# Moving a load-transpose-split step between two stages of a decoder kernel: memory tokens beside the first projections in place of beside the recurrence

## The chip, the cores and the metric

The kernel runs on one core of one Trainium2 chip. The time is the device time in microseconds (us) of one execution of the whole program; a smaller number is better. Five engines of the core matter here: TensorE (PE in the profile, with its weight loads as PEld), VectorE (DVE), ScalarE (ACT), GpSimd (POOL) and SyncE (SP). In this kernel SP computes nothing: it issues nearly all DMA transfers, and it issues them in the order in which they stand in its queue.

## The reference, cut to what matters

The program is one inference step of a two-layer decoder for a prompt of 1024 tokens and 8 sample tokens (one new token each). Layer 0 mixes tokens with a gated linear recurrence (4 heads) and, in parallel, with cross-attention into 256 memory tokens. Layer 1 uses another attention in place of the recurrence. The memory keys and values of both layers are projected once, from the same memory tokens:

```python
mk_p, mv_p = jnp.split(jnp.einsum('bmd,lde->lbme', mem_prompt, w_mem_kv), 2, axis=-1)

def a_mixer(hn, w_in, lb, hg_gain, mem_k, mem_v, w_o, s0):
    q_h, f_h, i_h, g_h, q_m = jnp.split(hn @ w_in, 5, axis=-1)
    q = jax.nn.silu(q_h)...
    logf = jnp.logaddexp(jnp.log(lb), jnp.log1p(-lb) + jax.nn.log_sigmoid(f_h...))
    k = -jnp.expm1(logf)
    v = i_h.reshape(B, L, HG_HEADS, HG_DV)
    o, S = hgrn2_scan(q, k, v, logf, s0)
    o = rmsnorm(o, hg_gain) * jax.nn.silu(g_h)
    om = mem_attend(q_m, mem_k, mem_v)
    out = jnp.concatenate([o, om], axis=-1) @ w_o
```

`mem_prompt` has 256 rows of 1024 numbers; `w_mem_kv` is 1024 by 1024 per layer (512 columns of keys, 512 of values). Everything is float32, and the results are wanted at float32 precision.

## The kernel before, in words

**Tokens and halves.** The 1024 prompt tokens are worked on in two halves of 512; the second half also carries the 8 sample tokens (520 columns). Activations stand transposed: features on the 128 partitions, tokens along the free dimension. In the code the first half is `a0` (layer 0) and `b0` (layer 1), the second `a1` and `b1`.

**Split products.** Every projection is done as three products of rounded numbers: an operand is split into a high part (a cast on ACT) and a low part (a subtraction on DVE), and PE adds high times high, high times low and low times high. `split_w` (L196 to L210) loads a 128x512 block of weights over SP into one of 5 `w` buffers (L201), casts it on ACT (L206) and subtracts on DVE (L207) into one of 5 `ws` buffers. `proj` (L212 to L223) then issues the matmuls (L220) into one of 2 `mm` buffers in PSUM. One head of a projection of the first half takes two such blocks and 24 matmuls.

**Memory tokens.** `mem_load` (L798 to L814) takes the memory tokens in two blocks of 128 rows. Each block comes over SP into a `c` buffer (L803), and is then treated in two groups. A group is four transposes on PE (L807) into the one `ns` bank of PSUM, and then two casts on ACT (L227) and two subtractions on DVE (L228) from that bank into the four `memt` tiles. There is only one `ns` bank, so the transposes of a group can start only when the four splits of the group before them have read it. `mem_keys` (L816) multiplies weight blocks with `memt` (L824, 24 matmuls a head), copies the result out (L829), stores it over SP (L830), transposes it back (L832, L834) and stores that too (L835). `mem_values` (L841) does likewise with L847, L848 and L851. Both need all of `memt` before they are finished, and the values of one layer need it from their first matmul on.

**The recurrence** of the first half is `hgrn_prompt` (L1145). For each of 4 heads it first prepares operands on ACT and DVE (L1158, L1159, L1164), multiplies on PE (L1168) and takes the result out on DVE (L1170, L1171) and decays on DVE (L1150 to L1152). After that come six levels with the matmuls of L1188, and a last part by heads (L1210 to L1237). It is a chain that goes to and fro between PE, DVE and ACT.

**What sets the order.** The program is written as generators, each `yield` being the end of a step. `drain` runs generators to their end, one after the other. `weave((gen, n), (gen, m))` takes steps from its generators in turn, so that each has made the same share of its given count. This order is the priority of the instructions. A planner then lays out one fixed queue for each engine: at each point of its own reckoning it takes the instruction of highest priority that it thinks ready. So an engine's queue can differ from the written order where the planner saw an engine free, but on the chip each engine goes through its queue in order and waits wherever the next instruction is not ready.

Around the change the order is: the value projection of the first half (`a0.v()`, L1042), the gate and query projections (`a0.fq()`: 4 heads of gates with L1073 to L1085 behind each, then 4 heads of queries with L237 to L241 behind each), then the recurrence (`a0.core()`) woven with one chain of memory load, keys, values, keys, values and the first half's memory queries (`a0.qm`).

Of the kernel before, what the change touches and what calls it, by code (L numbers as in the profile page):

```python
# [23 lines left out]
def tile_decoder(  # L24
# [25 lines left out]
    def nm(s):  # L50
        uid[0] += 1
        return f"{s}_{uid[0]}"
# [32 lines left out]
    def T(dt=F32):  # L85
        return tpool.tile([P, WID], dt, tag="t", name=nm("t"))
# [11 lines left out]
    def NS():  # L98
        return nsp.tile([P, 512], F32, tag="ns", name=nm("ns"))
# [18 lines left out]
    def C():  # L118
        return cpool.tile([P, 2, 512], F32, tag="c", name=nm("c"))
# [49 lines left out]
    def drain(*gens):  # L169
        for g_ in gens:  # L170
            for _ in g_:
                pass

    def chain(*gens):
        for g_ in gens:
            yield from g_

    def weave(*streams):

        live = [[0, n, g_] for g_, n in streams]  # L180
        while live:
            cur = min(live, key=lambda e: e[0] / e[1])
            cur[0] += 1
            try:
                next(cur[2])
            except StopIteration:
                live.remove(cur)
# [8 lines left out]
    def split_w(W, k0, nk, m0, alloc=None):  # L196
        out = []
        for a in range(0, nk, 4):
            n = min(4, nk - a)
            raw = wraw.tile([P, 4, P], F32, tag="w", name=nm("w"))  # L200
            nc.sync.dma_start(  # L201
                raw[:, :n, :],
                W[(k0 + a) * P : (k0 + a + n) * P, m0 : m0 + P].rearrange("(k p) m -> p k m", p=P),
            )
            ws = alloc() if alloc else wspl.tile([P, 2, 4, P], F32R, tag="ws", name=nm("ws"))
            nc.scalar.copy(ws[:, 0, :n, :], raw[:, :n, :])  # L206
            nc.vector.tensor_sub(ws[:, 1, :n, :], raw[:, :n, :], ws[:, 0, :n, :].bitcast(F32))  # L207
            for i in range(n):
                out.append((ws[:, 0, i, :], ws[:, 1, i, :]))
        return out  # L210
# [15 lines left out]
    def split_to(dst, src):  # L226
        nc.scalar.copy(dst[0], src)  # L227
        nc.vector.tensor_sub(dst[1], src, dst[0].bitcast(F32))  # L228
# [569 lines left out]
    def mem_load():  # L798
        memt.extend(xpool.tile([P, 2, 2, NM], F32R, tag="x1", name=nm("memt")) for _ in range(ND // 2))
        for tb in range(NM // P):  # L800
            xt = C()
            xf = xt.rearrange("p a n -> p (a n)")
            nc.sync.dma_start(xf, mem_prompt[0, tb * P : (tb + 1) * P, :])  # L803
            for a in range(0, ND, 4):
                ps = NS()
                for k in range(4):
                    nc.tensor.transpose(ps[:, k * P : (k + 1) * P], xf[:, (a + k) * P : (a + k + 1) * P], ident)  # L807
                for b in range(2):
                    d = memt[(a + 2 * b) // 2]
                    split_to(  # L810
                        (d[:, 0, :, tb * P : (tb + 1) * P], d[:, 1, :, tb * P : (tb + 1) * P]),
                        ps[:, 2 * b * P : (2 * b + 2) * P].rearrange("p (k t) -> p k t", k=2),
                    )
            yield  # L814

    def mem_keys(l):  # L816
        for h in range(H):
            w = split_w(w_mem_kv[l], 0, ND, h * P)
            pb = mmp.tile([P, 2, 512], F32, tag="mm", name=nm("mm"))
            ps, pt = pb[:, 0, :], pb[:, 1, :]  # L820
            for k in range(ND):
                wh, wl = w[k]
                for wi, (wt, xi) in enumerate(((wh, 0), (wh, 1), (wl, 0))):
                    nc.tensor.matmul(  # L824
                        ps[:, :NM], wt, memt[k // 2][:, xi, k % 2, :],
                        start=(k == 0 and wi == 0), stop=(k == ND - 1 and wi == 2),
                    )
            src = T()
            nc.scalar.copy(src[:, :NM], ps[:, :NM])  # L829
            nc.sync.dma_start(mks[l][:, h, :], src[:, :NM])  # L830
            for tb in range(2):
                nc.tensor.transpose(pt[:, tb * P : (tb + 1) * P], src[:, tb * P : (tb + 1) * P], ident)  # L832
            tok = T()
            nc.vector.tensor_copy(tok[:, :NM], pt[:, :NM])  # L834
            nc.sync.dma_start(  # L835
                mk_prompt[l, 0, :, h, :].rearrange("(t p) d -> p t d", p=P),
                tok[:, :NM].rearrange("p (t d) -> p t d", t=2),
            )
            yield

    def mem_values(l):  # L841
        pb = mmp.tile([P, 2, 512], F32, tag="mm", name=nm("mm"))
        for k in range(ND):
            raw = wraw.tile([P, 512], F32, tag="w", name=nm("w"))
            nc.sync.dma_start(raw, w_mem_kv[l][k * P : (k + 1) * P, H * P : 2 * H * P])
            ws = wspl.tile([P, 2, 512], F32R, tag="ws", name=nm("ws"))
            nc.scalar.copy(ws[:, 0, :], raw)  # L847
            nc.vector.tensor_sub(ws[:, 1, :], raw, ws[:, 0, :].bitcast(F32))  # L848
            for wi, (xi, i) in enumerate(((0, 0), (1, 0), (0, 1))):
                for tb in range(2):  # L850
                    nc.tensor.matmul(  # L851
                        pb[:, tb, :], memt[k // 2][:, xi, k % 2, tb * P : (tb + 1) * P], ws[:, i, :],
                        start=(k == 0 and wi == 0), stop=(k == ND - 1 and wi == 2),
                    )
            if k % 2 == 1 and k < ND - 1:
                yield
        tok = C()
        nc.scalar.copy(tok, pb)
        nc.sync.dma_start(mv_prompt[l, 0].rearrange("(t p) h d -> p t (h d)", p=P), tok)
        nc.sync.dma_start(mvs[l], tok)  # L860
        yield
# [613 lines left out]
    with tc.issue_after(made[0].ins):  # L1475
# [56 lines left out]
        nc.gpsimd.tensor_tensor(pidx, pidx, iot, op=ALU.add)  # L1532
    drain(head)
    a0 = mixer_a(0, x0)
    drain(a0.v(), a0.fq())
    weave(
        (a0.core(), 22),
        (chain(mem_load(), mem_keys(0), mem_values(0), mem_keys(1), mem_values(1), a0.qm(M)), 22),
    )
    a0.open()  # L1540
    a1 = mixer_a(1, x1)
# [94 lines left out]
```

## Time and profile before

| what | value |
|---|---|
| time, median of 3 runs | 2454.28 us (2452.27 to 2455.25) |
| the profiled execution | 2454.5 us |
| its span, from the first to the last instruction | 2452.8 us |
| PE busy | 2413.3 us (98% of the span) |
| PE weight loads busy | 2161.2 us (88%) |
| DVE busy | 1639.9 us (67%) |
| ACT busy | 1252.4 us (51%) |
| mean granted TensorE clock | 0.998 |
| first half's gate and query matmuls | about 39 to 83 us of the span |
| transposes of the memory tokens | from 84.6 us to 95.5 us |
| recurrence of the first half, PE's part | from 83.3 us to 186 us |

Times inside the span count from its start. PE is shown as busy for nearly all of it, so what can be had is where PE is not busy or where its granted clock is under 1. In the rows of an engine's timeline, the number in brackets at the end is the time the engine stood idle before, and the arrow names what it waited for. In the rows by window, the first number is the length of the window, and then come the busy times of PE, PEld, DVE, ACT and POOL with the number of their instructions, the granted clock, the busy share of the DMA engines and their GB/s.

### The profile page before, as it was taken

To read this page: it belongs to the slowest core of one execution; us is meant where nothing else is said; L and a number is where in the kernel's file an instruction comes from. 1 tells how busy PE (TensorE), PEld (TensorE's weight loads), DVE (VectorE), ACT (ScalarE), POOL (GpSimd) and SP (SyncE) were. 2 spreads that over 40 slices of the span, in tenths; PEclk is the share of its full clock that TensorE was granted. 3 is DMA by queue.
4 is the path that set the end of the run, shared out by engine and by line. 5 is a ranking of instruction groups with operands and counts; after the bars stand their busy time and mean duration, and the time that the engine had idled before them with its cause. 6 is when DMAs were issued, how large, how long until landed. Compare 5 with 4: busy or idle time off the path is not lost.

```text
span 2452.8 us, 42098 instructions
## 1 busy us (share of the span) xinstructions
PE 2413.3 (98%) x15839; PEld 2161.2 (88%) x15839; DVE 1639.9 (67%) x2987; ACT 1252.4 (51%) x2441; POOL 187.0 (8%) x315
## 2 busy tenths in 40 slices
PE   8999999999999999999999999999999999999998
PEld 6888889888879988999999989877777888999998
DVE  5766557665797686664756685788688467755565
ACT  5547644354445554555434554555554445654445
POOL 1000101111000000111200102121000100000000
PEclk9999999999999999999999999999999999999999
DMA  6354676567645447676766649745354563464542
GB/s 190 100 174 110 157 197 161 135 171 204 204 137 166 132 147 235 176 188 161 190 172 168 199 132 291 206 146 154 95 164 120 145 191 116 144 194 141 151 143 74
DMA packets 534733, 397.40 MB, mean 162 GB/s; under 512 B 21325, under 2 KB 473018, under 8 KB 534530
## 3 DMA queue, kind: packets, MB, share of 16 engines
q1 hardware_dynamic: 505346, 315.02, 43.2%
q0 software_dynamic: 29184, 79.70, 14.2%
q8 instruction: 124, 2.03, 0.3%
q14 instruction: 79, 0.65, 0.1%
HBM read 364.81 MB, written 101.14 MB: 190 GB/s over the span
## 4 chain that ended last, share of the span: by engine, by line
PE 84%; DVE 6%; DMA 5%; issue 2%; ACT 2%; POOL 0%; SPq 0%; DVEq 0%; ACTq 0%; POOLq 0%
PE mm L220 44%; PE q L511 13%; PE q L648 9%; PE q L464 3%; PE mm L1042 2%; PE s L1188 1%; DMA c<-in_cache_mem_v 1%; PE s L1385 1%; PE s L906 1%; PE mm L824 1%; PE mm L851 1%; PE q L680 1%; PE s L1351 1%; PE s L875 1%; DVE ws L207 1%
## 5 line engine op out<-in xcount | busy, mean ns | idle before, releaser
L220 PE MATMUL mm<-x,ws 128*128 128x260 f32 (+1 forms) x6240 | 1113.6, 335 | 4.9 <-DVE t L237 1.7
L220 PEld LDWEIGHTS mm<-x,ws 128*128 128x128 f32 x6240 | 941.8, 188 | 125.8 <-issue 2.4
L206 ACT CAST ws<-w 128x512 fp32r<-128x512 f32 (+1 forms) x652 | 382.3, 588 | 489.5 <-PE mm L220 337.0
L207 DVE TENSOR_TENSOR ws<-w,ws 128x512 fp32r<-128x512 f32 (+1 forms) x652 | 418.9, 648 | 246.8 <-ACT ws L206 241.7
L220 PE MATMUL mm<-m,ws 128*128 128x512 f32 (+1 forms) x1344 | 281.8, 361 | 0.1
L220 PEld LDWEIGHTS mm<-m,ws 128*128 128x128 f32 x1344 | 217.9, 189 | 36.8 <-issue 1.0
L648 PE MATMUL q<-m,ws 128*128 128x260 f32 (+1 forms) x1824 | 221.8, 283 | 0.0
L648 PEld LDWEIGHTS q<-m,ws 128*128 128x128 f32 x1824 | 218.9, 188 | 1.2 <-DVE t L534 0.4
L502 DVE TENSOR_TENSOR ws<-w,ws 128x512 fp32r<-128x512 f32 x181 | 124.0, 690 | 86.6 <-ACT ws L501 83.6
L501 ACT CAST ws<-w 128x512 fp32r<-128x512 f32 x181 | 111.8, 621 | 110.2 <-PE q L648 35.6
L511 PE MATMUL q<-x,ws 128*128 128x260 f32 (+1 forms) x1188 | 158.1, 282 | 0.0
L511 PEld LDWEIGHTS q<-x,ws 128*128 128x128 f32 x1188 | 148.7, 188 | 0.0
L511 PE MATMUL q<-y,ws 128*128 128x260 f32 x912 | 119.7, 284 | 0.4 <-ACT q L521 0.3
L511 PEld LDWEIGHTS q<-y,ws 128*128 128x128 f32 x912 | 113.7, 189 | 0.8 <-ACT q L521 0.5
L464 PE MATMUL q<-x,ws 128*128 128x260 f32 (+1 forms) x720 | 91.3, 284 | 0.2 <-DVE r L400 0.2
L464 PEld LDWEIGHTS q<-x,ws 128*128 128x128 f32 x720 | 88.4, 189 | 1.8 <-DVE r L400 0.5
L511 PE MATMUL q<-a,ws 128*128 128x260 f32 (+1 forms) x672 | 87.0, 282 | 0.0
L511 PEld LDWEIGHTS q<-a,ws 128*128 128x128 f32 x672 | 83.2, 188 | 0.0
L657 DVE TENSOR_TENSOR r<-r,q 128x260 f32<-128x260 f32 (+1 forms) x128 | 48.5, 420 | 50.5 <-PE q L648 50.5
L237 DVE TENSOR_SCALAR t<-mm 128x512 f32<-128x512 f32 (+1 forms) x58 | 40.1, 691 | 48.0 <-PE mm L220 47.8
L563 POOL COPY mk<-a 128x1 f32<-128x1 f32 x36 | 21.3, 592 | 645.5 <-ACT a L1241 392.9
L228 DVE TENSOR_TENSOR m<-t,m 128x512 fp32r<-128x512 f32 (+1 forms) x88 | 60.8, 691 | 9.4 <-ACT m L227 8.7
(355 smaller groups left out, 3029.5 us busy)
## 6 DMA issues: line engine op xcount, KB each, us to landing
w<-in_w_gu SPq DMA_DIRECT2D x297, 256.0 KB
w<-in_w_down SPq DMA_DIRECT2D x160, 256.0 KB
wsum<-in_w_gu POOLq DMA_DIRECT2D x72, 512.0 KB, 6.6
w<-wsum SPq DMA_DIRECT2D x104, 256.0 KB
w<-in_w_in_a SPq DMA_DIRECT2D x80, 256.0 KB
w<-in_w_o SPq DMA_DIRECT2D x64, 256.0 KB
wsum<-in_w_gu POOLq DMA_DIRECT2D x24, 640.0 KB, 7.3
wsum<-wsum POOLq DMA_DIRECT2D x24, 512.0 KB, 5.7
```

The costliest lines, as they stand in the source:

```text
L206: nc.scalar.copy(ws[:, 0, :n, :], raw[:, :n, :])
L207: nc.vector.tensor_sub(ws[:, 1, :n, :], raw[:, :n, :], ws[:, 0, :n, :].bitcast(F32))
L220: nc.tensor.matmul(ps[:, a, : PW[g]], wt, xt[k][:, xi, o : o + PW[g]], start=(k == 0 and wi == 0), stop=(k == nk - 1 and wi == 2),)
L228: nc.vector.tensor_sub(dst[1], src, dst[0].bitcast(F32))
L237: nc.vector.tensor_scalar(sv(x, g), pv(ps, g), -44.0, None, op0=ALU.max)
L464: ins = nc.tensor.matmul(pp[a][:, :h], wt, xt[k][:, xi, a * h : (a + 1) * h], start=(k == 0 and wi == 0), stop=(k == ND - 1 and wi == 2),)
L501: nc.scalar.copy(w[:, 0, :], src)
L502: nc.vector.tensor_sub(w[:, 1, :], src, w[:, 0, :].bitcast(F32))
L511: nc.tensor.matmul(ps[:, :h], w[:, wj, k * P : (k + 1) * P], x[:, xi, :], start=(first and k == 0 and wi == 0), stop=(k == 3 and wi == 2), ...
L648: nc.tensor.matmul(pp[a][:, :h], wt, mids[k][:, xi, a * h : (a + 1) * h], start=(k == 0 and wi == 0), stop=(k == nf - 1 and wi == 2),)
L657: nc.vector.tensor_add(d, d, pp[a][:, :h])
L1042: nc.tensor.matmul(pb[i][:, a, :], xt[k][:, xi, c * P : (c + 1) * P], ws[:, s, :], start=(k == 0 and wi == 0), stop=(k == ND - 1 and wi == 2),
```

## The change

`mem_load()` is taken out of the chain that is woven with the recurrence. It is woven with the gate and query projections instead, one of its two blocks for every four of their eight steps. With the counts given, the first block stands after the first gate head and the second after the fifth step (the first query head). The other weave keeps its remaining 20 steps, and its count goes from 22 to 20. No instruction is added or removed.

```diff
-    drain(a0.v(), a0.fq())
+    drain(a0.v())
+    weave((a0.fq(), 8), (mem_load(), 2))
     weave(
         (a0.core(), 22),
-        (chain(mem_load(), mem_keys(0), mem_values(0), mem_keys(1), mem_values(1), a0.qm(M)), 22),
+        (chain(mem_keys(0), mem_values(0), mem_keys(1), mem_values(1), a0.qm(M)), 20),
     )
```

## The prediction

> **What bounds the kernel now.** I read the page first, then the busy time by windows, then PE's own timeline where a window showed PE short.
>
> ```profile
> span 2452.8 us, 42098 instructions
> ...
> PE 2413.3 (98%) x15839; PEld 2161.2 (88%) x15839; DVE 1639.9 (67%) x2987; ACT 1252.4 (51%) x2441; POOL 187.0 (8%) x315
> ```
>
> PE is busy for all but 2452.8 - 2413.3 = 39.5 us of the span. An edit that leaves PE's work as it is can win only from those 39.5 us, and from stretches at a lower clock. The windows around the change:
>
> ```profile
> core 0: us, PE busy (x) PEld busy (x) DVE busy (x) ACT busy (x) POOL busy (x), PEclk, DMA share, GB/s
> 39.00:83.00 44.00, 44.00 (x192) 35.79 (x191) 28.45 (x46) 28.82 (x49) 0.00 (x0) 1.00 0.32 96
> 84.00:88.00 4.00, 1.40 (x11) 1.17 (x10) 4.00 (x11) 2.99 (x8) 0.00 (x0) 1.00 0.23 69
> 88.00:92.00 4.00, 3.34 (x14) 3.01 (x13) 2.24 (x6) 1.76 (x6) 0.00 (x0) 0.59 0.02 4
> 92.00:96.00 4.00, 3.35 (x23) 2.89 (x23) 3.42 (x9) 1.53 (x5) 0.00 (x0) 0.98 0.00 0
> 96.00:100.00 4.00, 4.00 (x33) 3.79 (x32) 3.82 (x10) 2.99 (x9) 0.00 (x0) 1.00 0.01 3
> ...
> 84.00:100.00 16.00, 12.09 (x75) 10.86 (x74) 13.48 (x35) 9.27 (x27) 0.00 (x0) 0.89 0.06 19
> 100.00:116.00 16.00, 16.00 (x132) 15.70 (x132) 15.44 (x40) 4.70 (x11) 0.00 (x0) 1.00 0.59 161
> ```
>
> The first row is the stage that the step moves to: PE never stops, DVE and ACT are idle for a third of it. Then the projections end, and from 84 to 100 us PE is short by 16.00 - 12.09 = 3.91 us, with the granted clock down to 0.59 in one of those four windows. PE's timeline names the waits (the last bracket is the idle time before the row and what ended it):
>
> ```profile
> 83.27 1.47 PE L1168 MATMUL s<-b,a 128*128 128x192 f32 x8
> 84.57 0.60 PE L807 MATMUL ns<-ident,c 128*128 128x128 f32 x4
> 87.77 0.63 PE L807 MATMUL ns<-ident,c 128*128 128x128 f32 x4 [2.60 <-DVE memt L228]
> 89.06 2.93 PE L1168 MATMUL s<-b,a 128*128 128x192 f32 x8 [0.66 <-ACT b L1164]
> 91.78 0.78 PE L807 MATMUL ns<-ident,c 128*128 128x128 f32 x4
> 93.02 0.51 PE L824 MATMUL mm<-memt,ws 128*128 128x256 f32 x2 [0.46 <-ACT memt L227]
> 93.72 1.22 PE L824 MATMUL mm<-memt,ws 128*128 128x256 f32 x8 [0.19 <-DVE memt L228]
> ```
>
> 2.60 + 0.66 + 0.46 + 0.19 = 3.91, so these four waits are the whole gap. Three of them are for the memory tokens: the second group of transposes waits until the splits of the first have left the one `ns` bank, and the key matmuls wait for `memt`. Meanwhile the key weights stand ready, and nothing else on PE is.
>
> **The price of the low clock.** The chain of waits gives the same eight matmuls of L1168 at both clocks, and two paces that I need below:
>
> ```profile
> 89.06 2.94 PE s L1168 x8
> ...
> 95.26 0.44 PE ns L807 x4
> ...
> 100.06 1.37 PE s L1168 x8
> ...
> 104.85 2.90 PE mm L824 x24
> ```
>
> 2.94 - 1.37 = 1.57 us. From the windows it is 3.34 x 0.41 + 3.35 x 0.02 = 1.44. I take 1.5. That the hole of 2.60 us is its cause is read from the order of the rows: the clock was 1.00 through the hole and low right after it. A smaller hole elsewhere did not do it:
>
> ```profile
> 540.00:560.00 20.00, 18.27 (x89) 14.60 (x89) 15.96 (x21) 8.36 (x15) 2.67 (x2) 1.00 0.85 243
> ```
>
> ```profile
> 557.43 4.79 PE L220 MATMUL mm<-x,ws 128*128 128x260 f32 x38 [1.73 <-DVE t L237]
> ```
>
> So after the change, holes of up to 1.73 us should leave the clock alone. [...]
>
> **The change, part by part.** *Removed from 84 to 97 us.* Sixteen transposes (L807, four groups at 0.44, 1.8 us of PE), eight casts and eight subtractions:
>
> ```profile
> L228 DVE TENSOR_TENSOR memt<-ns,memt 128x256 fp32r<-128x256 f32 x8 | 3.3, 414 | 0.6 <-ACT memt L227 0.6
> L227 ACT CAST memt<-ns 128x256 fp32r<-128x256 f32 x8 | 3.0, 369 | 5.5 <-PE ns L807 4.6 <-DVE memt L228 0.7
> ```
>
> *Added from 44 to about 72 us.* The same. On PE the 1.8 us are a wash: PE is full there, so what leaves one place is paid in the other. On DVE and ACT 3.3 and 3.0 us go into idle time of 44.00 - 28.45 = 15.55 and 44.00 - 28.82 = 15.18 us, so they cost nothing if the weight splits keep their lead. Without that cover they would cost 3.3 us at most.
>
> *Is there cover for PE at 83 us?* The splits made by then:
>
> ```profile
> L207 DVE TENSOR_TENSOR ws<-w,ws 128x512 fp32r<-128x512 f32 x20 | 13.8, 688 | 9.3 <-ACT ws L206 9.3
> L206 ACT CAST ws<-w 128x512 fp32r<-128x512 f32 x20 | 12.4, 621 | 14.0 <-PE mm L1042 6.7 <-PE mm L220 5.0 <-DMA w<-in_w_in_a 1.6
> ```
>
> These are the groups up to 83.4 us. The gate and query heads need 8 x 2 = 16 of the 20, so 4 blocks of key weights stand split, each good for 12 matmuls: 4 x 12 x 2.90 / 24 = 5.8 us of work that waits for `memt` alone. With `memt` there early, PE has more ready work than the 3.91 us that it idled, and each block it uses sets a `ws` buffer free some 10 us sooner than now. DVE then makes the next block in 0.69 us (13.8 / 20) against 1.45 us that PE needs for one.
>
> *The queues.* The loads of the memory tokens are moved in the order too, and so stand ahead of the weight loads of the gates. SP's queue and its waits:
>
> ```profile
> 10.39 0.91 SPq L803 DMA_DIRECT2D c<-in_mem_prompt  x2
> ...
> 60.46 19.20 SPq L201 DMA_DIRECT2D w<-in_w_mem_kv  x8
> 82.06 3.12 SPq L845 DMA_DIRECT2D w<-in_w_mem_kv  x2
> 99.12 0.33 SPq L830 DMA_DIRECT2D mks<-t  x1
> 99.60 0.33 SPq L845 DMA_DIRECT2D w<-in_w_mem_kv  x1
> ```
>
> ```profile
> SPq L830 <- ACT t L829: 19.3, 4, 13.9
> ```
>
> SP issued the two token loads at 10.39 us already, 34 us before the transposes could now want them, so I cost the loads at nothing; the `c` buffers they hold are freed sooner, not later. After 85.2 us SP stood for 13.9 us behind the store of the first key head (L830), with all weight loads behind it. That store comes sooner when the first key head does, so this wait shortens. POOL's queue is not touched: it has no instruction from 39 to 100 us.
>
> *New waits.* Two kinds that the trace does not price. First, the bank wait of the second group of each token block now stands in the projections' queue, where a stopped PE costs in full. Lower end: 0 each, as the planner may put projection matmuls between. Upper end: 2.60 each, the row above. Second, PE must take the key matmuls and the recurrence's first part by turns, and can stand before a head of L1168 that is not ready: from 0 (no wait from 96 to 100 us, where both alternate) to 0.66 for each of three heads. The nearest row for queues that were interleaved and miss by a little is the memory attention's:
>
> ```profile
> PE s L899 <- DVE b L892: 2.1, 7, 0.6
> ```
>
> 0.3 us a wait. I take 2 x 0.3 = 0.6 and 3 x 0.3 = 0.9, together 1.5, with 0 and 2 x 2.60 + 3 x 0.66 = 7.2 as ends.
>
> **The sum.** The profiled execution took 2454.5 us, 1.7 more than its span, and 0.2 more than the median of 2454.28. From 2454.3: minus 3.91 for the idle time, minus 1.5 for the clock, plus 1.5 for new waits gives 2450.4 us, 0.16% less. From no change a measurement of this kernel can tell about 0.2%, 4.9 us: under 2449.4 is faster, over 2459.2 slower. With the new waits at 0 the time is 2448.9. Holes in the rest of the program, 39.5 - 3.9 less 10.3 in the first 20 us (PE is busy for 9.71 us there), come to 25.3 us and may shift by 2 us or so when the planner's queues shift; that is a guess of size, not a row.
>
> ```profile
> 0.00:20.00 20.00, 9.71 (x48) 7.52 (x49) 12.92 (x36) 12.54 (x27) 6.74 (x27) 1.00 0.72 237
> ```
>
> **Rivals.**
> *All of it is won.* No new wait, and the later holes don't grow: 2448.9 us. For it: 5.8 us of split key weights against a gap of 3.91. Against: every change between engines in the rows above left some wait.
> *DVE sets the pace.* From 84 to 100 us DVE is busy 13.48 of 16, and from 100 to 116 us 15.44 of 16. If the recurrence and the key splits are held up by DVE, PE's hole closes early and opens again later, and only DVE's relief of 3.3 us is won: 2451.0 us. Against: PE is at 16.00 of 16.00 next to that full DVE.
> *The low clock stays.* The rows show it after the hole, not because of it. If it is not the hole's doing, only 3.91 - 1.5 is won: 2451.9 us. Against: the other windows above without such a hole have 1.00. [...]
> *The projections stall (slower).* The planner puts the second group of transposes close behind the first, and on the chip the four splits stand behind the gates' own chain on ACT and DVE. Then both waits are 2.60 us, each with its low clock of 1.5: 2454.3 - 5.4 + 0.9 + 8.2 = 2458.0 us. It decides from 5.4 - 0.9 = 4.5 us of such stalls on. For it: one `ns` bank, and 2.60 us once already. Against: here PE has 24 matmuls a head to put between, and at 89 us it did so with L1168. Anything worse than this, two longer stalls, passes 2459.2.
> *It does nothing.* The planner takes instructions when it thinks an engine free, and could leave the transposes about where they were: 2454.3 us. Against: they now rank ahead of seven projection heads, and their data is there.
>
> **Chances.** 2450.4 (0.44: 0.12 below 2449.4, 0.32 within 0.2%; its own range 2448.9 to 2452.5), all won 0.23 (faster), DVE's pace 0.10, the low clock stays 0.05, nothing 0.06 (all three within), stalls 0.12 (0.09 slower, 0.03 within). Faster 0.35, within 0.2% 0.56, slower 0.09. The range goes from 2447.0, all won and 2 us of later holes, to 2455.5, past the cases without stalls; I leave out most of the stalls and the luckiest shifts, under 2 in 10.
>
> **What would show it.** L807 between 44 and 72 us in groups of four among the rows of L220, with idle time before the second and fourth group of 0 to 0.6 us. From 39 to about 85 us PE without other holes, the end of the projections some 1.8 us later. Behind them L824 at once beside L1168, PE over 15 of 16 us busy in the next 16, and clock 1.00. SP's wait at L830 well under 13.9 us. The forecast is wrong if PE waits for L228 inside the projections by more than 1 us, if the low clock remains, or if a new hole stands between 100 and 220 us. From 100 to 330 us PE now waits for this alone, in the memory attention behind 230 us:
>
> ```profile
> PE s L899 <- DVE b L892: 0.6, 3, 0.2
> ```

## The result, and the profile after

The changed kernel takes 2446.55 us (median of 7 runs, 2445.13 to 2449.87); the kernel before, run beside it, 2455.08 us. The ratio is 0.9968, with a 95% interval of 0.9956 to 0.9979: faster by 0.32%, or 8 us, with 5 to 11 us as the bounds. The forecast was 2450.4 us, 0.16%, and gave "within 0.2%" the largest chance. The direction was right, the size was half of what was measured, and the median lies just under the range's low end of 2447.0.

The busy time by windows of the changed kernel, with the columns as before:

```profile
39.00:83.00 44.00, 43.99 (x199) 35.35 (x198) 30.15 (x52) 29.71 (x56) 0.00 (x0) 1.00 0.31 90
...
84.00:100.00 16.00, 16.00 (x116) 15.27 (x115) 14.55 (x35) 10.11 (x26) 0.00 (x0) 1.00 0.42 126
100.00:116.00 16.00, 16.00 (x111) 14.75 (x111) 14.95 (x39) 4.39 (x8) 0.00 (x0) 1.00 0.54 162
```

PE has no hole from 84 to 100 us any more (16.00 against 12.09 us busy), and its clock is 1.00. The projections stay full too. PE's timeline shows why:

```profile
45.36 0.60 PE L807 MATMUL ns<-ident,c 128*128 128x128 f32 x4
45.72 2.79 PE L220 MATMUL mm<-x,ws 128*128 128x512 f32 x11
48.51 0.63 PE L807 MATMUL ns<-ident,c 128*128 128x128 f32 x4
48.90 19.90 PE L220 MATMUL mm<-x,ws 128*128 128x512 f32 x85
68.63 0.60 PE L807 MATMUL ns<-ident,c 128*128 128x128 f32 x4
68.98 2.79 PE L220 MATMUL mm<-x,ws 128*128 128x512 f32 x11
71.78 0.63 PE L807 MATMUL ns<-ident,c 128*128 128x128 f32 x4
72.17 14.35 PE L220 MATMUL mm<-x,ws 128*128 128x512 f32 x61
86.35 1.47 PE L1168 MATMUL s<-b,a 128*128 128x192 f32 x8
87.52 3.13 PE L824 MATMUL mm<-memt,ws 128*128 128x256 f32 x24
```

Eleven projection matmuls (2.79 us) stand between the two groups of each token block, about as long as the second group waited for the `ns` bank before (2.60 us). No row has an idle time in brackets. At 87.52 us a whole key head runs at once. SP's wait behind the first key head's store fell from 13.9 us to 4.6 at most:

```profile
SPq L830 <- ACT t L829: 11.2, 5, 4.6
```

**Where the 8 us are.** Two marks of PE stand in both kernels: the first projection matmul (L220) and the transposes of the sample tokens (L339), behind the recurrence. In the kernel before, and then in the changed one:

```profile
38.91 2.47 PE L220 MATMUL mm<-x,ws 128*128 128x512 f32 x10
```

```profile
216.06 0.66 PE L339 MATMUL s<-ident,c 8*128 8x8 f32 x8
```

```profile
39.83 5.70 PE L220 MATMUL mm<-x,ws 128*128 128x512 f32 x24
```

```profile
210.64 0.66 PE L339 MATMUL s<-ident,c 8*128 8x8 f32 x8
```

From mark to mark it is 177.15 us before and 170.81 after: 6.3 us of the 8.2 by which the two spans differ. The first mark came 0.9 us later, and the rest of the program is 2.8 us shorter. The queues of all engines behind L339 hold the same instructions in the same order in both kernels, so those 2.8 us need another reason; the runs below look for it. Within the stretch, the time from each PE matmul's start to the next one's, summed by line (worked out from the trace's rows), moves like this:

| line | before | after | difference |
|---|---|---|---|
| L807, transposes of the memory tokens | 6.16 | 1.48 | -4.68 |
| L1168, recurrence's first part | 6.43 | 4.74 | -1.69 |
| L824, keys | 24.37 | 23.53 | -0.84 |
| L220, projections | 84.02 | 85.01 | +0.99 |
| all other lines | 56.18 | 56.05 | -0.13 |

By place: from the first L220 row to the first row of L1168 (83.27 us before, 86.35 after) the changed kernel takes 2.2 us more, and from there to L339 it takes 8.5 us less. Of the 0.99 on L220, 0.69 lies among the gate and query matmuls; the other 0.3 lies later, where no transpose of the memory tokens stands in either kernel.

### The profile page after: what moved, and what is told of

Its sections match the earlier page's. It is cut to its first block, busy times and chain, and to the rows that moved or that the text cites. A ratio compares the mean times of both kernels' runs of the same rounds, so it can differ in the third digit from the quotient of the medians.

```text
span 2444.6 us, 42106 instructions
## 1 busy us (share of the span) xinstructions
PE 2412.0 (99%) x15839; PEld 2159.3 (88%) x15839; DVE 1639.0 (67%) x2987; ACT 1251.2 (51%) x2441; POOL 186.1 (8%) x315
## 4 chain that ended last, share of the span: by engine, by line
PE 87%; DVE 6%; DMA 3%; issue 2%; ACT 2%; POOL 0%; SPq 0%; DVEq 0%; ACTq 0%; POOLq 0%
PE mm L220 46%; PE q L511 13%; PE q L648 9%; PE q L464 3%; PE mm L1042 2%; PE s L1188 1%; PE s L906 1%; PE s L1385 1%; PE mm L851 1%; PE mm L824 1%; PE s L875 1%; PE q L680 1%; PE s L1351 1%; DVE ws L207 1%; DMA b<-qd 1%
## 5 line engine op out<-in xcount | busy, mean ns | idle before, releaser
L220 PE MATMUL mm<-x,ws 128*128 128x260 f32 (+1 forms) x6240 | 1115.6, 335 | 3.5 <-DVE r L657 1.7
L220 PEld LDWEIGHTS mm<-x,ws 128*128 128x128 f32 x6240 | 941.0, 188 | 123.9 <-DVE x L228 2.1
L220 PE MATMUL mm<-m,ws 128*128 128x512 f32 (+1 forms) x1344 | 281.8, 361 | 0.5 <-DVE r L400 0.4
L220 PEld LDWEIGHTS mm<-m,ws 128*128 128x128 f32 x1344 | 217.8, 188 | 37.2 <-issue 1.0
L566 POOL DMA_DIRECT2D wsum<-in_w_gu x64 | 58.5, 935 | 114.1 <-DMA wsum<-wsum 89.5
```

The source lines that it names most:

```text
L220: nc.tensor.matmul(ps[:, a, : PW[g]], wt, xt[k][:, xi, o : o + PW[g]], start=(k == 0 and wi == 0), stop=(k == nk - 1 and wi == 2),)
L566: nc.gpsimd.dma_start(d, a, accum_op=ALU.add)
```

## The experiments

Each kernel was compared with the kernel before on its own chip. As single executions scatter by several us, I read the stretch from L220 to L339 in the profile as well, in which two profiles of the same kernel agree within 0.5 us: 177.2 and 177.7 for the kernel before, 170.8 and 170.9 for the changed one. The stretches below are taken from the starts of those two rows.

| kernel | ratio to before, 95% interval | L220 to L339, us |
|---|---|---|
| the change | 0.9968 (0.9956 to 0.9979) | 170.8 |
| filled hole | 0.9994 (0.9983 to 1.0004) | 175.7 |
| three banks | 1.0002 (0.9990 to 1.0014) | 176.4 |
| half moved | 0.9976 (0.9967 to 0.9986) | 172.6 |
| more transposes | 1.0022 (1.0012 to 1.0032) | 178.3 |
| load put back | 0.9984 (0.9974 to 0.9993) | 171.9 |
| one stage earlier | 0.9977 (0.9965 to 0.9988) | 168.7 (transposes ahead of it) |
| forced stall | 1.0001 (0.9991 to 1.0010) | 176.4 |
| no weave | 0.9980 (0.9971 to 0.9990) | 170.4 |

**Both kernels again.** No edit.

> The kernel before once more, to see what repeats. If the hole behind the projections belongs to the queues, PE is again short by 3.9 us (3.7 to 4.1) from 84 to 100 us, and the low clock stands there again if the hole causes it. The later differences between the two first profiles (1.5 us near 557 us, 0.7 us near 1480 us, 0.8 us near 1850 us, 3.0 us together) stand behind instructions whose order is the same in both kernels. Theory: they are chance of transfers, so this second profile of the same kernel differs from the first by 0.5 to 3 us in those places. Rival: they come from the change in some way that the order does not show, and then the same kernel repeats them within 0.3 us each.

> The changed kernel once more. Theory: PE has no hole from 84 to 100 us and its clock is 1.00 there; between the start of the projections' matmuls (L220) and the transposes of the sample tokens (L339) it takes 6.3 us less than the kernel before (6.0 to 6.6). The start of L220 may lie up to 1 us off the first profile in either direction, if that difference of 0.9 us is chance. Rival for the later places: the hole near 550 us is again 0.3 us and not above 1 us, if the change closed it.

The hole came back with three of its four waits (2.60, 0.67 and 0.46 us; the one of 0.19 did not), and so did its absence. The second pair differs by 6.8 us in the stretch, a little more than the 6.0 to 6.6 expected. In the later places the same kernel did not repeat itself. The hole of 1.73 us at 557 us was 0.66 in this profile of the kernel before:

```profile
558.03 5.98 PE L220 MATMUL mm<-x,ws 128*128 128x260 f32 x48 [0.66 <-DVE t L237]
```

In the changed kernel it was 0.28 and then 0.36, as the rival asked. But the kernels below, in which PE has the same order there, show anything from 0.58 to 3.52, so the change did not close it. From L339 to PE's last matmul it took 2229.6 and 2230.8 us before, 2226.9 and 2229.2 after, and the eight kernels below lie between 2227.7 and 2234.4. So the 2.8 us between the first two profiles are within what this part varies by itself; that the change adds something there isn't shown. The waits at 557 us go back to transfers: in the chain of waits of the first profile stand 7.85 us for a store of the sample states and 4.12 us for a load. The start of L220 was 40.1 us in this profile of before and 39.4 in that of after, the other way round than in the first pair, so that 0.9 us was chance too. One thing differed in the stretch: the low clock held for two windows where it had held for one.

```profile
88.00:92.00 4.00, 2.38 (x8) 2.01 (x9) 2.89 (x7) 2.05 (x7) 0.00 (x0) 0.56 0.02 7
92.00:96.00 4.00, 3.54 (x17) 3.02 (x16) 2.86 (x9) 0.76 (x3) 0.00 (x0) 0.59 0.01 4
```

**The hole filled, for the clock.**

```diff
+                if tb == 0 and a == 0:
+                    pj = S()
+                    for j in range(12):
+                        nc.tensor.matmul(pj, onesr, x0[j % ND][:, 0, :G], start=True, stop=True)
                 for b in range(2):
```

> The kernel before, with 12 matmuls of 512 columns that nobody reads behind the first group of the memory tokens' transposes, where PE stood for 2.60 us. They take 12 x 0.233 = 2.8 us. Theory that the hole causes the low clock: the clock stays 1.00 from 88 to 92 us, the next eight matmuls of L1168 take 1.4 us and not 2.9, and from 83 to 100 us the kernel is some 1.3 us quicker (1.5 for the clock less the 0.2 by which the filling is longer than the hole). Rival that the low clock is not the hole's: it remains 0.5 to 0.6 there, L1168 takes 2.9 us, and the kernel is 0.2 us slower. In the whole time neither can be told from 0 (0.1%).

```profile
85.64 3.03 PE L811 MATMUL s<-x,onesr 128*128 128x512 f32 x12
88.50 0.62 PE L807 MATMUL ns<-ident,c 128*128 128x128 f32 x4
89.33 1.57 PE L1172 MATMUL s<-b,a 128*128 128x192 f32 x8 [0.22 <-ACT b L1168]
```

```profile
88.00:92.00 4.00, 3.31 (x19) 2.29 (x17) 3.36 (x11) 1.95 (x7) 0.00 (x0) 1.00 0.01 4
```

With useless work in the hole the clock stays 1.00, the eight matmuls (here L1172) take 1.57 us in place of 2.93, and the stretch is 1.4 us shorter although PE does more. So the hole causes the low clock, at the price that was forecast.

**Three banks in place of one.**

```diff
-                ps = NS()
+                ps = S()
```

> The kernel before, with the memory tokens' transposes written into the three banks that the recurrence also uses, and not into the one ns bank. Theory that the one bank makes the hole: the second group follows the first at once, the wait of 2.60 us before it is gone, and with it the low clock: 3 to 4 us less. Rival that the chain behind it makes the hole (transposes, then eight casts and subtractions one behind the other, and only then key matmuls): the hole moves behind the second group, PE is short by 3 us or more from 84 to 100 us as before, and the gain is under 1 us.

```profile
85.89 0.63 PE L807 MATMUL s<-ident,c 128*128 128x128 f32 x4 [0.80 <-DVE b L1171]
88.87 2.22 PE L1168 MATMUL s<-b,a 128*128 128x192 f32 x8 [2.35 <-ACT b L1164]
```

The rival holds. The wait of 2.60 us is gone from the second group, and one of 2.35 us stands behind it, with the low clock (0.70 from 88 to 92 us). The stretch is 0.8 us shorter. So the bank named the wait, but it wasn't the reason: what came next on PE had to wait until ACT and DVE had gone through their queues. The test isn't a clean one, as the recurrence uses the three banks too (the wait of 0.80 us) and the third and fourth group stand behind L1168 in PE's queue.

**Half of it moved.**

```diff
-    drain(a0.v(), a0.fq())
+    drain(a0.v())
+    ml = mem_load()
+    weave((a0.fq(), 8), (islice(ml, 1), 2))
...
-        (chain(mem_load(), mem_keys(0), ..., a0.qm(M)), 22),
+        (chain(ml, mem_keys(0), ..., a0.qm(M)), 21),
```

> Only the first block of memory tokens is moved beside the projections; the second stays beside the recurrence. Theory that PE stood for want of ready work: key matmuls need both blocks, so PE still has none at 83 us and has to wait for the splits of the second block. With half the transposes and splits left, the hole is about half: 1.5 to 2.5 us idle from 84 to 100 us, and the gain is 2 to 3.5 us. Rival that the single bank alone counts: the wait between the first two groups is moved away and one between the last two is left, 2.4 us with other work beside it, so nearly all of the 6.3 us is won.

```profile
87.66 0.50 PE L824 MATMUL mm<-memt,ws 128*128 128x256 f32 x2 [0.79 <-ACT memt L227]
88.44 1.33 PE L824 MATMUL mm<-memt,ws 128*128 128x256 f32 x9 [0.28 <-DVE memt L228]
89.61 0.60 PE L807 MATMUL ns<-ident,c 128*128 128x128 f32 x4
```

The stretch is 4.6 us shorter, above the 2 to 3.5 expected, and 1.07 us of idle time is left. A key matmul takes one of the eight feature blocks of `memt`, and the planner ran those that were ready between the two last groups. With holes of 0.8 us the clock stays 1.00. The theory missed that the second block alone does not empty PE; the rival, which had nearly all of the 6.3 us won, missed the 1.07 us.

**More transposes, for their price.**

```diff
+                for _ in range(4):
+                    pj = S()
+                    for k in range(4):
+                        nc.tensor.transpose(pj[:, k * P : (k + 1) * P], xf[:, (a + k) * P : (a + k + 1) * P], ident)
```

> The changed kernel with each group of transposes followed by four more of the same that nobody reads, 16 groups (64 transposes) added beside the projections. It prices what a group costs on a full PE. By the pace inside a group (0.44 us) they add 16 x 0.44 = 7.0 us to the changed kernel. By what the first profile of the changed kernel shows, where each group takes 0.37 us and the projections lost another 0.25 us at each change between transposes and matmuls, they add 6 to 7 us if the groups stand together and 10 us if they stand apart. If the projections had idle time on PE, they would add clearly less than 6 us.

The 16 groups cost 178.3 - 170.9 = 7.4 us in the stretch, 0.46 each; they stood nearly together, and 0.45 us of the 7.4 are two waits for the `ns` bank. In the changed kernel the four groups stand apart and cost 1.48 on L807 and 0.69 on the projections around them, which is 0.54 each. So what moved is not free in its new place, and is no wash with 1.8 us either: it costs 2.2. In the whole time this kernel is 10 to 13 us above the changed one and those close to it (1.0022 against 0.9968 to 0.9980). What goes beyond the 7.4 us lies outside the stretch; a longer hole at 557 us, shown in the last section, is one part of it, and the rest is open.

**DVE's and ACT's load put back** into the changed kernel, for the rival that DVE sets the pace:

```diff
             nc.sync.dma_start(mks[l][:, h, :], src[:, :NM])
+            if l == 0:
+                for j in range(2):
+                    mj = M(F32R)
+                    split_to((mj[:, 0, :NM], mj[:, 1, :NM]), src[:, :NM])
```

> The changed kernel with eight casts and eight subtractions of 128x256 put back on ACT and DVE beside the recurrence, two of each behind every key head of layer 0, into tiles that nobody reads. So DVE and ACT have about the load back that the change took from them (3.3 and 3.0 us), and PE has nothing back. Theory that PE sets the pace there and DVE's relief is worth nothing: the time is that of the changed kernel, within 1 us from L1168 to L339. Rival that DVE sets the pace: up to 3.3 us slower than the changed kernel.

The stretch is 1.0 us longer than that of the changed kernel. The increase lies on L824 (24.79 against 23.53 by the sums of starts), and PE has no idle time between L1168 and L339 in either kernel. But PE's queue is not the same any more: with the added instructions the planner cut the key heads into pieces, where the changed kernel runs each as 24 matmuls at once.

```profile
91.23 3.62 PE L824 MATMUL mm<-memt,ws 128*128 128x256 f32 x28
95.65 0.42 PE L824 MATMUL mm<-memt,ws 128*128 128x256 f32 x1
96.47 3.02 PE L824 MATMUL mm<-memt,ws 128*128 128x256 f32 x23
```

By the whole time its interval overlaps that of the changed kernel. So DVE does not set the pace: with its load back, PE waits for nothing. Whether the 1.0 us comes from that load or from the other order of PE's queue is not shown.

**One stage earlier.**

```diff
-    drain(a0.v())
-    weave((a0.fq(), 8), (mem_load(), 2))
+    weave((a0.v(), 4), (mem_load(), 2))
+    drain(a0.fq())
```

> The memory tokens one stage earlier still: woven with the value projection. The transposes then stand between 20 and 37 us. Theory: PE is full there too, so the time is that of the changed kernel within 1 us, 6 us less than before; the hole at 84 us is closed in the same way. Rival: the splits meet the weight splits of the value projection, which have little lead there (each weight block is cast when its transfer lands), and PE waits for them: 1 to 3 us slower than the changed kernel.

From the first value matmul (L1042) to L339 it takes 195.5 us, against 195.9 and 195.6 in the two profiles of the changed kernel and 201.9 before. So between the two stages ahead that were tried the place does not matter. The earlier one brings no more either: PE is busy for 23.4 of the 24 us from 16 to 40 us in this kernel as in the kernel before.

**Stalls forced into the projections**, the slower rival of the prediction as a kernel:

```diff
-    weave((a0.fq(), 8), (mem_load(), 2))
+    fq, ml = a0.fq(), mem_load()
+    for n in (1, 4):
+        for _ in range(n):
+            next(fq)
+        next(ml)
+        with tc.issue_after(moved[0].ins):
+            next(fq)
+    drain(fq, ml)
```

Here `moved[0]` is the last transpose that `mem_load` issued.

> The changed kernel, with the next head's matmuls put behind the second group of each token block on PE's queue. So PE has nothing to put between the two groups and must stand until the four splits of the first have left the ns bank, twice, in the projections. This is the slower rival of the prediction, made on purpose. Each hole should be 2.3 to 2.7 us by the profile and cost 0.2 us more than that, as the end of the last matmul before it is shown inside its busy time. Theory that any such hole brings the low clock: 2 x (2.7 + 1.5) = 8.4 us more than the changed kernel from L220 to L339. Rival, that one hole of this length alone does not bring it (before, the hole stood in 4 us in which PE was busy for only 1.40 us): 5.4 us more, the clock stays 1.00.

```profile
44.56 0.60 PE L807 MATMUL ns<-ident,c 128*128 128x128 f32 x4
47.71 0.63 PE L807 MATMUL ns<-ident,c 128*128 128x128 f32 x4 [2.55 <-DVE memt L228]
...
80.80 0.63 PE L807 MATMUL ns<-ident,c 128*128 128x128 f32 x4 [1.43 <-DVE memt L228]
```

```profile
48.00:52.00 4.00, 4.00 (x15) 3.15 (x13) 2.61 (x6) 1.68 (x4) 0.00 (x0) 0.59 0.23 66
52.00:56.00 4.00, 4.00 (x19) 3.26 (x18) 0.69 (x1) 1.09 (x2) 0.00 (x0) 0.98 0.13 35
```

The first hole is as forecast and brings the low clock. Into the second the planner drew eight matmuls of the recurrence (L1168), which left 1.43 us of it, and the clock stayed. The stretch is 5.6 us longer than in the changed kernel: 2.55 + 1.43 idle and about 1.5 of clock. Nearly the whole gain is given back, at a ratio of 1.0001. So the rival's mechanism is real, and one full stall costs about what it said (2.55 and 1.5 us); the order on PE's queue decides whether it comes.

**Without the weave.**

```diff
-    drain(a0.v())
-    weave((a0.fq(), 8), (mem_load(), 2))
+    drain(a0.v(), mem_load(), a0.fq())
```

> The changed kernel, but with the memory step written as a whole between the value projection and the gate projections and not woven with them. Theory: the planner spreads the groups by itself, as the matmuls of the first gate head are ready while the bank is not, so the time is that of the changed kernel within 1 us (170.9 us from L220 to L339, less up to 0.5 us for a group that falls before L220). Rival that the weave keeps the groups apart: holes of up to 2.6 us between the groups, 2 to 5 us slower than the changed kernel.

```profile
39.96 0.60 PE L807 MATMUL ns<-ident,c 128*128 128x128 f32 x4
40.31 2.79 PE L220 MATMUL mm<-x,ws 128*128 128x512 f32 x11
42.94 0.60 PE L807 MATMUL ns<-ident,c 128*128 128x128 f32 x4
```

The planner spreads the groups by itself, with eleven matmuls between, and the stretch is 170.4 us. The weave is not what kept PE full; the ready matmuls were.

## Why the prediction was right and wrong

*The hole, right in place and cause.* PE's 3.91 us of idle time from 84 to 100 us were for work that the memory tokens hold back, and all of it went. Three banks did not help, half the move won 4.6 us, and every version with the tokens ahead of 83 us and no forced stall won 6 to 7: the reason is that PE had nothing else ready. I named the bank in the same breath as the reason; that part fell.

*The clock, right.* 1.5 us forecast, 1.4 measured by filling the hole. The rival "the low clock stays" is out. In the windows of the first profile of before, 0.41 x 4 + 0.02 x 4 = 1.7 us of clock are lost. In its trace that is one stretch of 3.41 us at 0.50, from 88.72 to 92.13 us; the second profile lost twice that, 0.44 x 4 + 0.41 x 4 = 3.4 us. Idle time of 2.55 us brought the low clock in the forced stall too.

*New waits, the step that failed first.* I took 1.5 us for two bank waits and three waits of the recurrence, by the row of the memory attention. They are 0: eleven matmuls fitted into each bank wait, and L1168 and L824 alternate from 86 to 104 us without one. In another order of the same queue such waits do come: the forced stall has 2.55 and 1.43 us of them, against the upper end of 2.60 each.

*The sum's idle term, mis-sized.* Behind the projections the sum took away 3.91 us of idle time, 1.5 for the clock and 1.8 for the transposes: 7.2 us. From the first row of L1168 to L339 it was 8.5. About 0.7 of the 1.3 us that are missing lies on the transposes: their 6.16 us less 3.72 of idle time and 4 x 0.44 of pace. The idle time of a row begins at the end of the last matmul, and a group of transposes fills 0.60 us in the timeline and 0.44 in the chain, so a wait costs some 0.2 us more than it shows. Most of the rest lies on the key matmuls (0.84 less 0.19 of idle time), which stood in small pieces before; no run takes that apart. *The wash, wrong:* 1.8 us forecast for the transposes in the projections, 2.2 measured. Together 8.5 - 2.2 = 6.3 us, where the sum without new waits has 3.91 + 1.5 = 5.4.

*Cover and queues, right.* The split weights were there, SP's longest wait at L830 fell from 13.9 to 4.6 us, and ACT and DVE took the splits without a wait on PE.

*DVE's pace*, 0.10 of the chance, is not borne out: with the load back the stretch grew by 1.0 us of the 3.3, and PE had no wait there.

*The range.* From 2454.3 us the stretch alone gives 2448.0, or 0.26%. That is already beyond 0.2%; with waits of 0 my own sum gave 2448.9, and that case should have had the larger chance. What lies between 6.3 us and the measured 8 is not settled: the interval of 5 to 11 us holds both, and the rest of the program varies by more. The two kernels with the same gain in the stretch, one stage earlier and no weave, came out only 5 to 6 us below the kernel before, so part of the 8 may be chance.

## What to carry to other kernels

Where one engine is full everywhere but in one hole, look for what that hole's work waits for, and move its small preparations into the stage ahead, where other engines have idle time; both stages ahead that were tried had it (DVE was busy for 28.45 of 44 us in the one and for 12.76 of 24 us in the other) and won 6 to 7 us. A bank or semaphore named at the hole need not be its reason: ask what else the engine had ready. Price a hole by the starts of the instructions on both sides, and add the clock where PE does little around it: here 1.7 us, behind a step of 3.41 us in which PE was busy for 0.63 us.

## What the hardware showed that was not expected

The length of a hole alone does not decide whether the low clock follows. One and the same wait stands near 1694 us in the kernel before and near 1687 us in the changed one. The rows are from the second profile of the kernel before, from its first, and from the second of the changed kernel:

```profile
1694.96 1.16 PE L1385 MATMUL s<-b,a 128*128 128x128 f32 x8 [1.79 <-ACT b L1382]
```

```profile
1693.48 1.16 PE L1385 MATMUL s<-b,a 128*128 128x128 f32 x8 [1.55 <-ACT b L1382]
```

```profile
1687.18 1.16 PE L1385 MATMUL s<-b,a 128*128 128x128 f32 x8 [1.95 <-ACT b L1382]
```

After 1.79 us the clock was 0.57 in the next window; after 1.55 it was 1.00, as after 1.73 at 557 us, and it was 1.00 after 1.95 too, the longest of these. What the traces show in its place is a fixed step of time. From the first record of the clock on, it changes only at whole steps of 3.41 us in all twelve traces, and it stays low for one step or two. In the first profile of the kernel before the record begins at 13.63 us; the clock falls at 88.72, 22 steps on, is 0.50 for one step, and then 1.00 for 690 steps, until it falls at the end. In that of the changed kernel it is 1.00 for 710 steps, from 16.57 to 2440.03 us. Two such steps each, from the second profile of the kernel before and from the second of the changed kernel:

```profile
1692.71:1696.12 3.41, 1.62 (x11) 1.15 (x11) 2.91 (x5) 2.59 (x5) 0.00 (x0) 1.00 0.82 276
1696.12:1699.53 3.41, 3.41 (x10) 2.41 (x8) 2.52 (x4) 1.15 (x2) 1.61 (x2) 0.50 0.23 85
```

```profile
1683.51:1686.93 3.42, 1.72 (x8) 1.07 (x6) 3.42 (x6) 1.52 (x3) 0.00 (x0) 1.00 0.62 173
1686.93:1690.34 3.41, 3.05 (x17) 2.27 (x18) 2.91 (x5) 2.00 (x5) 0.51 (x1) 1.00 0.64 215
```

The hole of 1.95 us lay across two steps. Up to the last 15 us of the program, the clock fell after each of the seven steps at full clock in which PE was busy for less than 1.5 us (0.63 us from 85.31 us on, in the first profile of the kernel before), after one of the five with 1.5 to 1.9, and after none with more. (At the program's very end it fell after more: after 2.03 us in the first profile of the kernel before, where PE had only the transposes of L753 and the matmuls of one column of L768.) So in these traces the share of a step that PE is busy goes with the fall, and a hole of some 2 us cost its length alone (1.95 us) or about 1.7 us more (1.79 us, then a step of 3.41 us at 0.50), by where it lay.

In the kernel with more transposes the hole at 557 us grew to 3.52 us, and the clock was 0.66 and 0.91 in the two windows of 4 us behind it, which is 1.7 us lost:

```profile
560.67 5.59 PE L220 MATMUL mm<-x,ws 128*128 128x260 f32 x32 [3.52 <-DVE t L237]
```

So this wait, which goes back to transfers, cost its length, and in this profile 1.7 us more. That fits with how single executions of one kernel scatter: of 31 of the kernel before on one chip, the 13 with a mean clock of 0.999 took 2453.5 us on average, and the five with 0.997 took 2459.1.
